# Scores of a gated linear attention: products of 64 rows, one a head, in place of pairs beside zeros

## The chip, the core and the metric

One core of a Trainium2 chip runs the whole program. The metric is the device time of one execution in microseconds. The kernel before was timed in three runs: 610.01, 610.43 and 611.85, the median being 610.43. The execution whose profile is read here took 611.44.

## What is computed

One layer of a hybrid decoder over 512 tokens of 1024 channels: a mixer (gated linear attention beside a short convolution), a mixture of 16 experts, a gate with per-layer embeddings, and a last norm, all in float32. The change lies in the attention: 4 heads, keys of 64 channels, values of 128. Cut to what matters:

```python
def step(state, inp):
    qc, kc, vc, ac = inp
    cum = jnp.cumsum(ac, axis=2)
    o_inter = jnp.einsum('bhld,bhde->bhle', qc * jnp.exp(cum), state)
    diff = cum[:, :, :, None, :] - cum[:, :, None, :, :]
    decay = jnp.exp(jnp.where(causal, diff, -jnp.inf))
    scores = jnp.einsum('bhtd,bhsd,bhtsd->bhts', qc, kc, decay)
    o_intra = jnp.einsum('bhts,bhse->bhte', scores, vc)
```

The decay differs by channel, so a score is not a plain product of q and k.

## The kernel before

Tokens stand in chunks of 128 (NT = 4). Heads are held in pairs (`pr` = 0 or 1): partitions 0 to 63 hold the one head's channels, 64 to 127 the other's, tokens along the free axis. `qT`, `kT` and `cum` are such tiles of 128x512, one a pair.

Scores are made by levels `b` = 1, 2, 4 to 64. At a level each block of 2b tokens falls into an earlier and a later half; the decay between a key of the earlier and a query of the later half goes by way of the boundary, so it is a product of a factor of the key and one of the query. `lev_sub` (POOL) takes the differences of `cum`, `lev_exp` (ScalarE) their exponentials `F`, and `lev_mul` (VectorE) multiplies the keys' halves by `kT` in place (line 537) and writes the queries' halves, times `qT`, to another tile (line 540). `scores(b, cc)` then makes the products for two of the four chunks on TensorE (line 549): the stationary operand is `F` of a chunk, 128 channels by 128 tokens, the moving one the chunk's 64 later-half queries. Since the stationary operand holds both heads of a pair, the queries are laid out as 128 columns: 64 of the one head, with zeros in the other head's partitions, and 64 of the other head, with zeros in the first one's. The tile for that, `qz`, lies in the right halves of the tiles that held x (xs in the trace), twice over for alternate levels; POOL writes its zeros once (`zero_q`, lines 495 and 496). Line 552 copies the products into the score tile `scs` under a mask (VectorE).

Two scores calls a level make 14. They don't stand alone. `merged` writes one projection step (12 products of 128x512, line 445) and then one or more of the side steps, and so sets the order by hand:

```python
merged(proj_steps([f"pC{i}" for i in range(4)], c_out), gla[:8])
merged(proj_steps([f"pu{i}" for i in range(4)], u_out), gla[8:16])
merged(proj_steps([f"pg{i}" for i in range(4)], g_out), gla[16:] + tail + [nop] * 2)
```

The first two give one side step to each projection step, the third two or three. The products of the scores, the diagonal (line 566, 2 columns) and other small ones take their PSUM banks in turn from a pool of four (`aux_ps`); a new tile waits until what read the fourth before it is done. The projections have four banks of their own.

Each projection's weights come as float32, and are split into a high and a low part by ScalarE (line 117) and VectorE (line 118): three products a weight. `Stream` holds them: a transfer starts when a slot of its ring comes free, a split when TensorE has used an earlier one (`pump`).

Three other places matter below. Line 468 (`decay1`) makes pz from an operand of 16 rows, between projections. Line 614 (`o_mm`) multiplies the state, 64 rows a head, `hf` being the half of the partitions, each half to its own bank. Line 681 (`u_out`) writes `cu` on VectorE from the projection pu; line 811 is a product of the later embedding part, where TensorE also waits for a register (line 1168). The experts (line 1111) follow the mixer.

Of the kernel before, what the change touches and what calls it, by code (L numbers as in the profile page):

```python
# [23 lines left out]
NP = 2  # L24
# [13 lines left out]
HALF = 512  # L38
# [4 lines left out]
def merged(main, side):  # L43

    done = 0
    for i, step in enumerate(main):
        step()
        while done < (i + 1) * len(side) // len(main):
            side[done]()
            done += 1  # L50
# [101 lines left out]
def hymba_layer(ctx, tc, x, p, g_mix, w_in, w_gla_gate, b_gla_gate, g_gla_out, w_conv, w_out,  # L152
# [4 lines left out]
    p, w_in, w_out = p[0, 0], w_in[0], w_out[0]  # L157
    ve, se, pe, ge, sy = nc.vector, nc.scalar, nc.tensor, nc.gpsimd, nc.sync
# [18 lines left out]
    def aux_ps(name):  # L177
        return psa.tile([P, HALF], F32, tag="aux", name=name)

    def half(i):  # L180
        return slice(i * HALF, (i + 1) * HALF)

    def tok(t):
        return slice(t * P, (t + 1) * P)
# [11 lines left out]
    def X(t):  # L196
        return xt[t // 2][:, (t % 2) * D:(t % 2 + 1) * D]
# [55 lines left out]
    def t2k(name, dt=F32):  # L253
        return t2.tile([P, HALF], dt, tag="t2", name=name)

    def txk(name, dt=F32):
        return tx.tile([P, HALF], dt, tag="tx", name=name)
# [175 lines left out]
    def proj_steps(names, done):  # L433

        ws, dst = [], []

        def step(k):
            if k == 0:
                dst.extend(mm_ps(n_) for n_ in names)
            if k % 2 == 0:  # L440
                ws.extend(W.take())
            wh, wl = ws[k]
            for c in range(4):
                for n, (a, b_) in enumerate(((wh, hTh), (wl, hTh), (wh, hTl))):
                    pe.matmul(dst[c], a[:, tok(c)], b_[:, k, :], start=(k + n == 0), stop=(k == NK - 1 and n == 2))
                if k == NK - 1:
                    done(c, dst[c])
            if k % 2:
                W.done()
                W.pump()  # L450
        return [lambda k=k: step(k) for k in range(NK)]


    qT, kT, cum = [], [], []
# [11 lines left out]
    def decay1(pr):  # L466
        pz = aux_ps(f"pz{pr}")
        pe.matmul(pz, wg[:, tok(pr)], aT, start=True, stop=True)
        ab, m = dc[pr] = txk(f"ab{pr}"), txk(f"m{pr}")
        se.activation(ab, pz, AF.Abs, bias=bgla[:, pr:pr + 1])  # L470
        ve.tensor_scalar(m, pz, bgla[:, pr:pr + 1], 0.0, op0=OP.add, op1=OP.min)

    def decay2(pr):
        ab, m = dc[pr]
        se.activation(ab, ab, AF.Exp, scale=-1.0)
        se.activation(ab, ab, AF.Ln, bias=ones[:, 0:1])
        ve.tensor_sub(m, m, ab)
        cu = t2k(f"cum{pr}")
        ve.tensor_tensor_scan(cu, cmask.rearrange("p c t -> p (c t)"), m, 0.0, op0=OP.mult, op1=OP.add)
        cum.append(cu)  # L480

    def a_all():
        pa = aux_ps("pa")
        for t in range(NT):
            a_tr(t, pa)
        ve.tensor_copy(aT, pa[:RANK, :])

    qz = [[X(2 * i + pr)[:, half(1)].rearrange("p (c h t) -> p c h t", h=2, t=64) for pr in range(NP)]
          for i in range(2)]
    two = mc.tile([P, 2], F32, name="two")  # L490

    def zero_q():
        for i in range(2):
            for pr in range(NP):
                ge.memset(qz[i][pr][0:64, :, 1, :], 0.0)
                ge.memset(qz[i][pr][64:128, :, 0, :], 0.0)
        ge.memset(two, 0.0)
        ge.memset(two[0:64, 0:1], 1.0)
        ge.memset(two[64:128, 1:2], 1.0)

    merged(proj_steps([f"qk{j}" for j in range(4)], qk_out),
           [a_all, zero_q, lambda: decay1(0), lambda: decay1(1), lambda: decay2(0), lambda: decay2(1)])

    scs = ring.tile([P, 2 * D], F32, tag="raw3", name="scs")
    sc = [scs[:, c * HALF:(c + 1) * HALF].rearrange("p (h t) -> p h t", t=P) for c in range(NT)]
    idb = ident[:, None, :].to_broadcast([P, 4, P])

    fac = {}  # L510
    lv = (1, 2, 4, 8, 16, 32, 64)

    def lview(z, b):
        return z.rearrange("p (g u b) -> p g u b", u=2, b=b)

    def later_half(z, b):
        return z.rearrange("p (c n u b) -> p c n u b", c=NT, u=2, b=b)[:, :, :, 1, :]
# [13 lines left out]
            se.activation(Fq, Fq, AF.Exp, scale=1.0 / TAU)  # L531

    def lev_mul(b):
        R = qz[lv.index(b) % 2]
        for pr in range(NP):
            fv = lview(fac[b][pr], b)
            ve.tensor_mul(fv[:, :, 0, :], fv[:, :, 0, :], lview(kT[pr], b)[:, :, 0, :])
            for hf in range(2):
                hs = slice(64 * hf, 64 * hf + 64)
                ve.tensor_mul(R[pr][hs, :, hf, :].rearrange("p c (n b) -> p c n b", b=b),  # L540
                              later_half(fac[b][pr][hs], b), later_half(qT[pr][hs], b))

    def scores(b, cc):
        R = qz[lv.index(b) % 2]
        pl = aux_ps(f"pl{b}_{cc}").rearrange("p (c h t) -> p c h t", c=2, t=64)
        for i in range(2):
            c = 2 * cc + i
            for pr in range(NP):
                pe.matmul(pl[:, i, 2 * pr:2 * pr + 2, :], fac[b][pr][:, tok(c)], R[pr][:, c], start=True, stop=True)
        for i in range(2):  # L550
            n = 64 // b
            ve.copy_predicated(sc[2 * cc + i].rearrange("p h (n u b) -> p h n u b", u=2, b=b)[:, :, :, 1, :],
                               masks[b].rearrange("p (n b) -> p n b", b=b)[:, None].to_broadcast([P, 4, n, b]),
                               pl[:, i].rearrange("p h (n b) -> p h n b", b=b))

    qk = {}

# [86 lines left out]
    def o_out(c):  # L644
        ve.scalar_tensor_tensor(to[c], to[c], ggla, osq[c], op0=OP.mult, op1=OP.mult)

    gla = [lambda: (diag_mul(0), diag_mul(1), lev_sub(1)), lambda: (lev_sub(2), lev_exp(1)),
           lambda: (diag(0), lev_sub(4), lev_exp(2), lev_mul(1)), lambda: diag(1)]
    for j, b in enumerate(lv):
        def first(j=j, b=b):  # L650
            scores(b, 0)
            if j + 2 < len(lv):
                lev_exp(lv[j + 2])
            if j + 1 < len(lv):
                lev_mul(lv[j + 1])

        def second(j=j, b=b):
            scores(b, 1)
            if j + 3 < len(lv):
                lev_sub(lv[j + 3])  # L660
        gla += [first, second]
# [364 lines left out]
    t = NT - 1  # L1026
# [451 lines left out]
    for t in range(NT):  # L1478
        n = t + 1
# [15 lines left out]
    t = NT - 1  # L1495
# [12 lines left out]
    for i, c in enumerate(cols[1:]):  # L1508
        for k in range(NK):
            (xh, xl), (wh, wl) = x2T[t][k], wq[1][k]  # L1510
            for n, (a, b_) in enumerate(((xh, wh), (xh, wl), (xl, wh))):
                pe.matmul(pgl[i][:, :256], a, b_[:, 256 * i:256 * i + 256], start=(k + n == 0),  # L1512
                          stop=(k == NK - 1 and n == 2))
# [7 lines left out]
    c = cols[2]  # L1521
# [37 lines left out]
```

## Time and profile before

| | |
|---|---|
| Median of three runs | 610.43 us (610.01 to 611.85) |
| The profiled execution's own time | 611.44 us |
| Its span, first to last instruction | 609.7 us |
| Mean granted TensorE clock | 0.992 of 2.4 GHz |
| Busy: TensorE products, its loads, VectorE, ScalarE, GpSimd | 590.3, 452.6, 480.4, 364.7, 112.6 us |
| The line of the score products | 112 records, 14.8 us, from 80.3 to 127.2 us |
| HBM read | 137.03 MB |

PE is TensorE's stream of products, PEld its loads of stationary operands, which overlap the stream; DVE is VectorE, ACT ScalarE, POOL GpSimd. The ends of products are modelled: their starts are what to read. An f32 product appears as two loads and two products, so the 56 products of line 549 appear as 112; after fp32r operands (the projections) one product is one record. A shape such as 64*128 is rows by columns of the stationary operand.

### The profile page before, as it was taken

To read this page: it belongs to the slowest core of one execution; us is meant where nothing else is said; L and a number is where in the kernel's file an instruction comes from. 1 tells how busy PE (TensorE), PEld (TensorE's weight loads), DVE (VectorE), ACT (ScalarE), POOL (GpSimd) and SP (SyncE) were. 2 spreads that over 40 slices of the span, in tenths; PEclk is the share of its full clock that TensorE was granted. 3 is DMA by queue.
4 is the path that set the end of the run, shared out by engine and by line. 5 is a ranking of instruction groups with operands and counts; after the bars stand their busy time and mean duration, and the time that the engine had idled before them with its cause. 6 is when DMAs were issued, how large, how long until landed. Compare 5 with 4: busy or idle time off the path is not lost.

```text
span 609.7 us, 8447 instructions
## 1 busy us (share of the span) xinstructions
PE 590.3 (97%) x3030; PEld 452.6 (74%) x3030; DVE 480.4 (79%) x804; ACT 364.7 (60%) x518; POOL 112.6 (18%) x147
## 2 busy tenths in 40 slices
PE   7999999999999999899999999999999999989994
PEld 6997888887687788677777777777777777666884
DVE  4742799874395476799999999999999998879763
ACT  5532537203714333678877878877787898776322
POOL 1440664100420000123210111111011100000111
PEclk9999999999999999899999999999999999999998
DMA  8632222221126958599999999999999999991001
GB/s 281 215 105 70 69 70 69 70 79 61 55 83 219 384 187 310 174 388 363 379 374 363 357 360 343 377 375 359 346 344 351 376 319 378 360 359 75 35 34 70
DMA packets 65292, 146.15 MB, mean 240 GB/s; under 512 B 5205, under 2 KB 5804, under 8 KB 65246
## 3 DMA queue, kind: packets, MB, share of 16 engines
q1 hardware_dynamic: 61342, 136.16, 61.3%
q0 software_dynamic: 3744, 9.15, 6.3%
q8 instruction: 24, 0.39, 0.2%
q10 hardware_dynamic: 160, 0.27, 0.1%
q14 instruction: 22, 0.18, 0.1%
HBM read 137.03 MB, written 12.19 MB: 245 GB/s over the span
## 4 chain that ended last, share of the span: by engine, by line
PE 53%; DVE 3%; ACT 2%; issue 1%; POOLq 0%; DVEq 0%; ACTq 0%
PE pg L1111 14%; PE pd L1111 14%; PE pu L1111 13%; PE pgate L1111 5%; PE pt_xT L1099 2%; PE pp L811 1%; PE pgate_last L1512 1%; DVE lo L113 1%; PE pt_hT L1099 1%; DVE lo L118 1%; ACT hi L112 1%; PE px L1418 1%; PE pz L1246 0%; PE pslot L926 0%; ACT L1382 0%
## 5 line engine op out<-in xcount | busy, mean ns | idle before, releaser
L113 DVE TENSOR_TENSOR lo<-raw,hi 128x1024 fp32r<-128x1024 f32 x172 | 203.3, 1218 | 14.1 <-ACT hi L112 14.0
L112 ACT CAST hi<-raw 128x1024 fp32r<-128x1024 f32 x172 | 170.5, 1053 | 0.3 <-DMA raw<-in_w_exp_up_dram 0.3
L118 DVE SCALAR_TENSOR_TENSOR lo<-raw,cst,hi 128x512 fp32r<-128x512 f32 (+1 forms) x56 | 44.8, 843 | 17.7 <-ACT hi L117 17.5
L1081 POOL DMA_INDIRECT xe<-xgd,rowi x12 | 19.4, 1613 | 165.0 <-PE pt_xT L1099 158.7
L113 DVE TENSOR_TENSOR lo<-x,hi 128x1024 fp32r<-128x1024 f32 x30 | 36.0, 1218 | 1.7 <-ACT hi L112 1.7
L117 ACT ACTIVATE hi<-raw,cst 128x512 fp32r<-128x512 f32 (+1 forms) x56 | 36.7, 717 | 0.5 <-DMA raw<-in_w_in_dram 0.5
L1132 POOL DMA_INDIRECT xd<-ye,rowi x15 | 22.5, 1501 | 49.0 <-ACT ye L1305 45.4
L112 ACT CAST hi<-x 128x1024 fp32r<-128x1024 f32 x30 | 30.8, 1052 | 0.0
L1111 PE MATMUL pg<-hi,xT_1h 128*96 128x512 f32 x60 | 24.4, 407 | 0.0
L1111 PE MATMUL pg<-hi,xT_0h 128*96 128x512 f32 x60 | 23.7, 395 | 0.0
L1111 PE MATMUL pg<-lo,xT_1h 128*96 128x512 f32 x60 | 23.6, 394 | 0.0
L1111 PE MATMUL pg<-hi,xT_1l 128*96 128x512 f32 x60 | 23.5, 392 | 0.0
L1111 PE MATMUL pg<-lo,xT_0h 128*96 128x512 f32 x60 | 23.5, 392 | 0.0
L1111 PE MATMUL pg<-hi,xT_0l 128*96 128x512 f32 x60 | 23.5, 391 | 0.0
L1111 PE MATMUL pu<-hi,xT_0h 128*96 128x512 f32 x56 | 22.9, 409 | 0.0
L1111 PE MATMUL pu<-lo,xT_0h 128*96 128x512 f32 x56 | 22.1, 395 | 0.0
L1111 PE MATMUL pu<-lo,xT_1h 128*96 128x512 f32 x56 | 22.1, 394 | 0.0
L1111 PE MATMUL pu<-hi,xT_1h 128*96 128x512 f32 x56 | 22.1, 394 | 0.0
L1111 PE MATMUL pu<-hi,xT_1l 128*96 128x512 f32 x56 | 22.0, 392 | 0.0
L1111 PE MATMUL pu<-hi,xT_0l 128*96 128x512 f32 x56 | 21.9, 392 | 0.0
L636 ACT ACTIVATE sq<-xs 128x512 f32<-128x512 f32 x4 | 2.5, 630 | 28.5 <-DVE xs L618 28.5
L728 POOL TENSOR_TENSOR xs<-xs,sg 128x128 f32<-128x128 f32 x16 | 11.3, 738 | 44.2 <-ACT sg L723 44.1
(583 smaller groups left out, 1598.0 us busy)
## 6 DMA issues: line engine op xcount, KB each, us to landing
raw<-in_w_exp_gate_dram SPq DMA_DIRECT2D x28, 1024.0 KB, 16.8
raw<-in_w_exp_down_dram SPq DMA_DIRECT2D x27, 1024.0 KB, 13.9
raw<-in_w_exp_up_dram SPq DMA_DIRECT2D x26, 1024.0 KB, 18.1
raw<-in_w_in_dram SPq DMA_DIRECT2D x10, 1024.0 KB, 5.0
x<-in_w_exp_up_dram SPq DMA_DIRECT2D x6, 1024.0 KB, 13.5
x<-in_w_exp_down_dram SPq DMA_DIRECT2D x5, 1024.0 KB, 16.0
xs<-in_x_dram SPq DMA_DIRECT2D x16, 256.0 KB, 5.6
raw<-in_w_out_dram SPq DMA_DIRECT2D x4, 1024.0 KB
```

Source lines behind the costliest of these rows:

```text
L112: self.nc.scalar.copy(hi, rw)
L113: los.append(lambda: eng.tensor_sub(lo, rw, hi.bitcast(F32)))
L117: self.nc.scalar.activation(hi[:, c_], rw[:, c_], AF.Copy, scale=g_)
L118: los.append(lambda c_=c_, g_=g_: eng.scalar_tensor_tensor(lo[:, c_], rw[:, c_], g_, hi[:, c_].bitcast(F32), op0=OP.mult, op1=OP.subtract))
L728: ge.tensor_tensor(tv, tv, sgs[i][:, tok(t)], op=OP.mult)
L811: pe.matmul(pps_[i], a[:, tok(t)], b_[:, half(ci)], start=(k + n == 0), stop=(k == 1 and n == 2))
L1081: ge.indirect_dma_start(out=x_, out_offset=None, in_=xgd, in_offset=bass.IndirectOffsetOnAxis(ap=idx, axis=0), bounds_check=S - 1, oob_is_ ...
L1099: pe.transpose(pt[:, k * n:(k + 1) * n], src[:n, tok(k)], ident[:n, :n])
L1111: pe.matmul(dst, a, b_, start=(k + n == 0), stop=(k == nk - 1 and n == 2))
L1132: ge.indirect_dma_start(out=xd, out_offset=bass.IndirectOffsetOnAxis(ap=idx, axis=0), in_=y_, in_offset=None, bounds_check=S - 1, oob_is_e ...
L1418: pe.transpose(pt[:, tok(k)], X(t)[:, ci * HALF + k * P:ci * HALF + (k + 1) * P], ident)
L1512: pe.matmul(pgl[i][:, :256], a, b_[:, 256 * i:256 * i + 256], start=(k + n == 0), stop=(k == NK - 1 and n == 2))
```

## The change

The pair's zeros go. The queries' tile becomes `qd`, 256 columns (4 chunks of 64) over all 128 partitions, written by one product a pair in place of two of 64 partitions. `scores` makes one product a head, chunk and pair of it: rows 0 to 63 of the operands into bank `pl[0]`, rows 64 to 127 into bank `pl[1]`. So a call has 8 products of 64 rows and 64 columns in place of 4 of 128 and 128, and takes two banks in place of one. The copy goes by half (all chunks and pairs of a call from one bank) in place of by chunk; there are two a call as before. `zero_q` becomes `make_two`, without the eight memsets.

```diff
-    qz = [[X(2 * i + pr)[:, half(1)].rearrange("p (c h t) -> p c h t", h=2, t=64) for pr in range(NP)]
+    qd = [[X(2 * i + pr)[:, HALF:HALF + 256].rearrange("p (c t) -> p c t", t=64) for pr in range(NP)]
           for i in range(2)]
...
-    def zero_q():
-        for i in range(2):
-            for pr in range(NP):
-                ge.memset(qz[i][pr][0:64, :, 1, :], 0.0)
-                ge.memset(qz[i][pr][64:128, :, 0, :], 0.0)
+    def make_two():
...
     def lev_mul(b):
-        R = qz[lv.index(b) % 2]
+        R = qd[lv.index(b) % 2]
...
-            for hf in range(2):
-                hs = slice(64 * hf, 64 * hf + 64)
-                ve.tensor_mul(R[pr][hs, :, hf, :].rearrange("p c (n b) -> p c n b", b=b),
-                              later_half(fac[b][pr][hs], b), later_half(qT[pr][hs], b))
+            ve.tensor_mul(R[pr].rearrange("p c (n b) -> p c n b", b=b), later_half(fac[b][pr], b),
+                          later_half(qT[pr], b))
 
     def scores(b, cc):
-        R = qz[lv.index(b) % 2]
-        pl = aux_ps(f"pl{b}_{cc}").rearrange("p (c h t) -> p c h t", c=2, t=64)
+        R = qd[lv.index(b) % 2]
+        pl = [aux_ps(f"pl{b}_{cc}_{hf}")[:, :256].rearrange("p (q t) -> p q t", t=64) for hf in range(2)]
         for i in range(2):
             c = 2 * cc + i
             for pr in range(NP):
-                pe.matmul(pl[:, i, 2 * pr:2 * pr + 2, :], fac[b][pr][:, tok(c)], R[pr][:, c], start=True, stop=True)
-        for i in range(2):
-            n = 64 // b
-            ve.copy_predicated(sc[2 * cc + i].rearrange("p h (n u b) -> p h n u b", u=2, b=b)[:, :, :, 1, :],
+                for hf in range(2):
+                    hs = slice(64 * hf, 64 * hf + 64)
+                    pe.matmul(pl[hf][:, 2 * i + pr, :], fac[b][pr][hs, tok(c)], R[pr][hs, c], start=True, stop=True)
+        n = 64 // b
+        sv = scs[:, 2 * cc * HALF:2 * (cc + 1) * HALF].rearrange("p (q h n u b) -> p q h n u b", h=2, n=n, u=2, b=b)
+        for hf in range(2):
+            ve.copy_predicated(sv[:, :, hf, :, 1, :],
                                masks[b].rearrange("p (n b) -> p n b", b=b)[:, None].to_broadcast([P, 4, n, b]),
-                               pl[:, i].rearrange("p h (n b) -> p h n b", b=b))
+                               pl[hf].rearrange("p q (n b) -> p q n b", b=b))
```

How the order moves. On TensorE, around the first level's second call, before (pl is the scores' bank, xs the tile of the queries, F the factors of one pair, pC a projection's bank):

```order
L445 MATMUL pC_772<-hTh,hi 128x512
L445 MATMUL pC_772<-hTh,lo 128x512
L445 MATMUL pC_772<-hTl,hi 128x512
L549 MATMUL pl_1_926<-xs_79,F_0_789 128x128
L549 MATMUL pl_1_926<-xs_79,F_1_792 128x128
...
L445 MATMUL pC_769<-hTh,hi 128x512
```

and with the change:

```order
L445 MATMUL pC_764<-hTh,hi 128x512
L445 MATMUL pC_764<-hTh,lo 128x512
L445 MATMUL pC_764<-hTl,hi 128x512
L545 MATMUL pl_1_0_919<-xs_79,F_0_781 128x64
L545 MATMUL pl_1_1_920<-xs_79,F_0_781 128x64
L545 MATMUL pl_1_0_919<-xs_79,F_1_784 128x64
L545 MATMUL pl_1_1_920<-xs_79,F_1_784 128x64
...
L445 MATMUL pC_761<-hTh,hi 128x512
```

Each pair's product becomes two, one to each of two banks, and the products on both sides of the call, the projections', have 128 rows where these have 64. At the marks the same rows follow once more, for the call's second chunk. Thirteen calls lie so between projections. The last level's two calls, the 13th and 14th, stand back to back, with the change as before:

```order
L445 MATMUL pg_1282<-hTl,hi 128x512
L545 MATMUL pl_0_0_1295<-xs_79,F_0_1141 128x64
...
L545 MATMUL pl_0_1_1296<-xs_79,F_1_1144 128x64
L545 MATMUL pl_1_0_1307<-xs_79,F_0_1141 128x64
...
L545 MATMUL pl_1_1_1308<-xs_79,F_1_1144 128x64
L445 MATMUL pg_1279<-hTh,hi 128x512
```

So there are thirteen stretches of score products, the last one twice as long.

On VectorE, from the first call's copies to the next ones, before:

```order
L552 COPY_PREDICATED scs<-mask_158,pl_0_893 128x256 x2
L537 TENSOR_TENSOR F_0_813<-F_0_813,qkT_746 128x128x2
L540 TENSOR_TENSOR xs_80<-F_0_813,qkT_736 64x4x64 x2
L537 TENSOR_TENSOR F_1_816<-F_1_816,qkT_751 128x128x2
L540 TENSOR_TENSOR xs_80<-F_1_816,qkT_741 64x4x64 x2
L118 SCALAR_TENSOR_TENSOR lo<-raw_672,cst,hi 128x512 x2
L552 COPY_PREDICATED scs<-mask_158,pl_1_926 128x256 x2
```

and with the change:

```order
L549 COPY_PREDICATED scs<-mask_158,pl_0_0_883 128x4x64
L549 COPY_PREDICATED scs<-mask_158,pl_0_1_884 128x4x64
L533 TENSOR_TENSOR F_0_805<-F_0_805,qkT_738 128x128x2
L534 TENSOR_TENSOR xs_80<-F_0_805,qkT_728 128x256
L533 TENSOR_TENSOR F_1_808<-F_1_808,qkT_743 128x128x2
L534 TENSOR_TENSOR xs_80<-F_1_808,qkT_733 128x256
L118 SCALAR_TENSOR_TENSOR lo<-raw_664,cst,hi 128x512 x2
L549 COPY_PREDICATED scs<-mask_158,pl_1_0_919 128x4x64
L549 COPY_PREDICATED scs<-mask_158,pl_1_1_920 128x4x64
```

Two half-height products a pair become one of full height, and nothing changes its place. ScalarE's and SyncE's rows stay in number and order; GpSimd's lose the eight memsets.

## Rows read from the trace of the kernel before

**Rows 1.** Page, part 1: busy us (share of the span) xinstructions.

```profile
PE 590.3 (97%) x3030; PEld 452.6 (74%) x3030; DVE 480.4 (79%) x804; ACT 364.7 (60%) x518; POOL 112.6 (18%) x147
```

**Rows 2.** Busy by stretches: PE, PEld, DVE, ACT, POOL (xinstructions), clock, DMA share, GB/s.

```profile
60.00:135.00 75.00, 74.53 (x387) 62.56 (x386) 65.36 (x112) 30.75 (x52) 27.36 (x36) 1.00 0.22 71
...
260.00:560.00 300.00, 296.43 (x1462) 210.59 (x1461) 278.98 (x380) 240.48 (x306) 47.84 (x30) 1.00 0.99 352
```

**Rows 3.** TensorE's waits: line, releaser, us in total, times, longest.

```profile
PE pp L811 <- DVEq L1168: 1.5, 1, 1.5
...
PE pB L445 <- ACT sg L723: 0.9, 1, 0.9
...
PE pg L445 <- DVE cu L681: 0.3, 1, 0.3
```

**Rows 4.** Timeline, PE at the second call: start us, us, engine, line, xcount.

```profile
83.75 0.39 PE L445 MATMUL pC<-hTl,hi 128*128 128x512 f32 x1
83.98 1.05 PE L549 MATMUL pl<-xs,F 128*128 128x128 f32 x8
...
84.76 0.28 PE L549 MATMUL pl<-xs,F 128*128 128x128 f32 x1
84.79 0.48 PE L445 MATMUL pC<-hTh,hi 128*128 128x512 f32 x1
85.11 0.41 PE L445 MATMUL pC<-hTh,lo 128*128 128x512 f32 x1
```

**Rows 5.** Timeline, the loads (PEld) of the same call.

```profile
83.76 1.09 PEld L549 LDWEIGHTS pl<-xs,F 128*128 128x128 f32 x8
84.76 0.19 PEld L445 LDWEIGHTS pC<-hTh,hi 128*128 128x128 f32 x1
```

**Rows 6.** Timeline, seven of the loads of the diagonal's products (2 columns).

```profile
72.92 0.86 PEld L566 LDWEIGHTS pdg<-two,qkd 128*128 128x128 f32 x7
```

**Rows 7.** Timeline, line 614: the first four and all eight; two and four loads.

```profile
141.79 0.49 PE L614 MATMUL po<-Ec,S 64*128 64x128 f32 x4
...
141.79 0.71 PE L614 MATMUL po<-Ec,S 64*128 64x128 f32 x8
...
141.78 0.19 PEld L614 LDWEIGHTS po<-Ec,S 64*128 64x128 f32 x2
...
141.78 0.30 PEld L614 LDWEIGHTS po<-Ec,S 64*128 64x128 f32 x4
```

**Rows 8.** Timeline, the entry to line 468's products of 16 rows.

```profile
50.58 0.39 PE L445 MATMUL qk<-hTl,hi 128*128 128x512 f32 x1
50.90 1.12 PE L468 MATMUL pz<-aT,wg 16*128 16x512 f32 x2
...
50.90 0.29 PEld L468 LDWEIGHTS pz<-aT,wg 16*128 16x128 f32 x2 [0.36 <-issue]
```

**Rows 9.** Timeline, the exit from line 614's last pair.

```profile
151.37 0.28 PE L614 MATMUL po<-Ec,S 64*128 64x128 f32 x2
...
151.91 0.39 PE L445 MATMUL pg<-hTh,lo 128*128 128x512 f32 x1
...
151.57 0.19 PEld L445 LDWEIGHTS pg<-hTh,hi 128*128 128x128 f32 x1
```

**Rows 10.** VectorE by line, 60 to 135 us: xcount, busy us, mean ns, idle before.

```profile
L540 DVE TENSOR_TENSOR xs<-F,qkT 64x256 f32<-64x256 f32 x28 | 16.1, 574 | 0.2
L552 DVE COPY_PREDICATED scs<-mask,pl 128x256 f32<-128x256 uint8 x28 | 12.5, 531 | 3.0 <-PE pl L549 2.9
L537 DVE TENSOR_TENSOR F<-F,qkT 128x256 f32<-128x256 f32 x14 | 7.2, 517 | 0.2
```

**Rows 11.** Line 495 on POOL: ns min/median/max, first and last start (four of eight).

```profile
L495 POOL MEMSET xs<- x4: 304/306/308, 34.4 to 36.5; 64x256 f32 x4
```

**Rows 12.** Timeline, the second and third calls' copies, and the fourth call.

```profile
89.55 2.48 DVE L552 COPY_PREDICATED scs<-mask,pl 128x256 f32<-128x256 uint8 x4
91.83 1.05 PE L549 MATMUL pl<-xs,F 128*128 128x128 f32 x8
```

**Rows 13.** Busy by stretches, columns as in rows 2: the stretch after line 811's wait.

```profile
249.00:252.50 3.50, 3.50 (x10) 2.71 (x9) 2.51 (x15) 1.69 (x5) 0.67 (x1) 0.52 0.79 214
```

More of the change, by code (lines that the diff above doesn't have):

```diff
@@ L501, in hymba_layer @@
     merged(proj_steps([f"qk{j}" for j in range(4)], qk_out),
-           [a_all, zero_q, lambda: decay1(0), lambda: decay1(1), lambda: decay2(0), lambda: decay2(1)])
+           [a_all, make_two, lambda: decay1(0), lambda: decay1(1), lambda: decay2(0), lambda: decay2(1)])
     scs = ring.tile([P, 2 * D], F32, tag="raw3", name="scs")
```

## The prediction

> **What bounds the kernel now.** I read the page's busy shares first: TensorE's products fill 97% of the span, VectorE 79% [rows 1]. Shares are averages, so next comes the view by stretches: from 60 to 135 us, where all score products lie, PE is busy for 74.53 of 75 us and VectorE for 65.36; in the experts, 260 to 560 us, PE for 296.43 of 300 [rows 2]. Then TensorE's own waits: after 60 us only a few stand there, the largest 1.5 us for a register that VectorE's chain feeds (line 1168), then 0.9 us and 0.3 us [rows 3]. So TensorE's stream sets the end, from the scores to the last expert. A microsecond added to that stream moves the end by one; a microsecond taken off VectorE moves it only where one of those waits is for VectorE. The expert weights do not soften this: their transfers start when ring slots come free, and TensorE's progress frees those.
>
> **What one call of `scores` costs TensorE today.** A 128-row call is eight records (an f32 product shows as two loads and two streams, x8 for four products). The pC product before the call starts at 83.75, the first score product at 83.98, the next pC at 84.79 and the one after it at 85.11 [rows 4]. From pC to second pC that is 1.36 us. The first of the eight starts at 83.98 and the last at 84.76, so they come every 0.11 us. The loads run ahead: the first one goes out at 83.76, while pC still streams, and the load of the next pC at 84.76, together with the last score product [rows 5]. Nothing is lost at either edge.
>
> **What paces these products.** The diagonal's products have only 2 columns, and seven loads span 0.86 us with 0.19 each, so they still come every (0.86 - 0.19) / 6 = 0.11 us [rows 6]. The load of 128 columns is the floor; a shorter stream does not lower it.
>
> **What 64-row products cost.** The kernel already has some: line 614 multiplies the state in the same order (first half, second half, first half, second half), each half to its own bank, x24 records. Four of its records end 0.49 us after the first start, eight end 0.71 us after: two pairs in 0.22, a pair every 0.11 us [rows 7]. So the two halves do run side by side. Their loads do so too: two loads take 0.19 in all, and the second pair adds 0.11 (0.30 - 0.19) [rows 7]. A load of 64 rows therefore takes as long as one of 128 rows; what is gained is that two go at once.
>
> The change's call has 16 records in 8 pairs. A pair streams 64 columns where line 614 streams 128, so its stream is half as long (0.05 us), and the load's 0.11 sets the pace. **Eight pairs at 0.11 take what eight products at 0.11 took: no gain on TensorE.** The Trainium skill, "TensorEngine Tiling (Array Packing)", section "Theoretical Speedup", would have it otherwise: up to 2 times for a dimension of 64 or less. By that rule the sum below would be 14 x 8 x 0.055 = 6.2 us lower; the loads of the diagonal and of line 614 speak against it here.
>
> **What the change of the array's shape costs.** Entry: where a pz product of 16 rows follows a stream of 128 rows, its load does not run ahead. The 128-row product starts at 50.58, pz's two loads lie from 50.90 to 51.19 with 0.19 each, so the second goes out at 51.00 as the first product begins to stream [rows 8]. That is 0.43 us after the 128-row product; in today's call it is 83.98 - 83.75 = 0.23. Entry costs 0.20 more. Exit: the last pair of line 614 starts at 151.37, the load of the next 128-row product goes out only at 151.57, and the second product after it starts at 151.91 [rows 9]: 0.54, where today it is from the last score product (84.76) to 85.11, thus 0.35. Line 614's last pair streams 128 columns; a pair of 64 saves 0.05 of that, so exit costs 0.14 more. Together 0.34 us a call. The Trainium skill, the same page, section "Key Properties", says that a change of the tiling mode, not of the tile alone, drains TensorE; it gives no price.
>
> The 14 calls form 13 islands, since the last two stand back to back and the mode doesn't change between them: 13 x 0.34 = **+4.4 us**. Bounds: if the exit saves nothing for its shorter stream, 0.39 x 13 = +5.1; if the pairs come at 0.107 rather than 0.111, the 112 pairs give back 0.4, and with an exit another 0.05 cheaper, 4.4 - 0.4 - 0.65 = +3.4 remains.
>
> **The other parts.** VectorE loses 14 instructions: 28 products of 64x256, 574 ns on average, 16.1 us, become 14 of 128x256, for which the 14 products of line 537 are the nearest row, 517 ns on average, 7.2 us [rows 10]; some 9 us less. Only the 0.3 us that TensorE waits for `cu` gains, because the last level's products stand right before the `cu` products: -0.3. The rest is cover that grows. The copies stay 28, of as many elements; now they take four 64-column pieces of one half out of one bank. If the new pattern ran at half speed, 12.5 us more [rows 10] would come to VectorE and 9 would have gone, inside the 9.6 us it has free in this stretch [rows 2]. The eight memsets on POOL (306 ns each) lie at 34 to 37 us, long before anyone reads the tiles [rows 11]: nothing.
>
> The banks: a call now holds two of four, so a call waits until the copies of the call two before are done, where four were allowed. The tightest place is the fourth call, at 91.83. The four copies from 89.55 to 92.03 belong to the second and third calls; the second's are done at about 90.8 [rows 12], 1.0 us ahead. The two removed multiplications before them add over a microsecond to that. So this wait is taken as nothing; if it bit, it would be some tenths of a call, not of all calls.
>
> **The sum.** +4.4 - 0.3 = +4.1 us. On the profiled execution, 611.44 us (span 609.7 and 1.7 around it), that is 615.5; that execution stands 1.0 above the median of the three runs, 610.43. I forecast for the median: **614.5 us**, 0.7% slower. A measurement of this kernel can tell 0.3%, 1.8 us, from no change.
>
> One piece swings by itself: after the 1.5 us wait, the granted clock is 0.52 in 249 to 252.5 us [rows 13], nearly all of it at 1.2 of 2.4 GHz, which costs about 0.48 x 3.5 = 1.7 us. The three runs, 610.01 to 611.85, spread as wide. I don't know whether a stretch that arrives 4 us later keeps it.
>
> **Rivals.**
> 1. *The edges are hidden* (no change, chance 0.07). If the drain at entry or exit ran under something that the 16-row and line-614 rows lack, only pace would count, and that is equal: 610.43 - 0.3 = 610.1. Against it: both edges show a load that waits some 0.2 us beyond the last product's start, at both kinds of place where the shape changes.
> 2. *The stream sets the pace, not the load* (faster, 0.05). If a 64-row load cost half, a pair would come every 0.056 us: 14 x 8 x 0.055 = 6.2 us less, 614.5 - 6.2 = 608.3. It decides for faster once a pair comes in under 0.058 us (4.1 + 1.8 = 5.9, over 112 pairs = 0.053 off 0.111). For it: columns are halved. Against: the diagonal's loads hold 0.11 with 2 columns. The skill's rule of 2 times is this rival.
> 3. *The halves don't run side by side here* (slower still, 0.05), so the change's pairs are none: 112 more steps of 0.11 us, +12.4, thus 627. For it: nothing but the shorter stream; line 614 has the same order and the same two banks.
>
> **How the numbers follow.** My forecast has 0.83. Its own bounds are 610.43 + 3.4 - 0.3 - 1.7 = 611.8 (cheap edges, the slow stretch gone) and 610.43 + 5.1 + 1.4 = 616.9 (dear edges, no gain at `cu`, and 1.4, as the upper of the three runs stands above their median). The three rivals with 0.17 lie outside, and some 0.03 of the forecast's tails: the range is 611.8 to 616.9. Slower by over 0.3%: 0.82 of the forecast and rival 3, 0.87. Within 0.3%: rival 1 and 0.01 of the forecast, 0.08. Faster: rival 2, 0.05.
>
> **What would show it.** In the profile after: score records 224 in place of 112, two at a time (their 16 records span about 1.0 us); the first load of a call about 0.32 us after the pC product before it, not together with it; the load of the next pC about 0.15 us after the last pair; from pC to the second pC about 1.70 us where 1.36 stood; VectorE's busy time in this stretch down by some 9 us with no gain in the span; every later stage later by about 4 us and as long as before. I would be wrong if pairs came every 0.06 us (rival 2), if the loads still ran ahead (rival 1), if the 16 records spanned 1.9 us (rival 3), or if TensorE waited for VectorE at the start of calls, the banks' doing.

## The result, and the profile after

The changed kernel takes 613.80 us in the median of six runs (613.17 to 615.83), the kernel before, in six runs beside it, 610.84 (609.66 to 611.85). The ratio is 1.0056, its 95% interval 1.0043 to 1.0069: slower by 3.4 us (2.6 to 4.2). The two medians alone stand 2.96 us apart, inside that interval. The forecast was 4.1 us.

The busy shares on the page of the changed kernel, beside [rows 1]:

```profile
PE 592.2 (97%) x3142; PEld 450.5 (74%) x3142; DVE 468.7 (77%) x790; ACT 364.9 (60%) x518; POOL 108.1 (18%) x139
```

VectorE works 11.7 us less in all, TensorE's products 1.9 more. The stretches of the changed kernel, with the columns of [rows 2]:

```profile
60.00:135.00 75.00, 75.00 (x483) 59.57 (x482) 51.72 (x94) 30.53 (x51) 25.30 (x36) 1.00 0.22 71
...
249.00:252.50 3.50, 2.01 (x15) 1.44 (x14) 1.83 (x14) 2.39 (x3) 1.88 (x2) 1.00 0.15 29
```

From 60 to 135 us TensorE now counts as never idle, and VectorE is idle for 23 of 75 us, in part because some of its work has moved past 135 us. TensorE's 75.00 hides what the change costs: the modelled end of a product reaches over the gap behind it, so what a call loses shows only in the starts. Next the timeline of TensorE's products at the second call, beside [rows 4]:

```profile
83.64 0.40 PE L445 MATMUL pC<-hTl,hi 128*128 128x512 f32 x1
83.97 1.11 PE L545 MATMUL pl<-xs,F 64*128 64x64 f32 x16
85.01 0.50 PE L445 MATMUL pC<-hTh,hi 128*128 128x512 f32 x1
85.35 0.40 PE L445 MATMUL pC<-hTh,lo 128*128 128x512 f32 x1
```

and of its loads, beside [rows 5]:

```profile
83.97 0.97 PEld L545 LDWEIGHTS pl<-xs,F 64*128 64x128 f32 x16 [0.37 <-issue]
85.00 0.19 PEld L445 LDWEIGHTS pC<-hTh,hi 128*128 128x128 f32 x1
```

From pC to second pC it is 85.35 - 83.64 = 1.71 us, where 1.36 stood. The sixteen loads go out two at a time, (0.97 - 0.19) / 7 = 0.11 us a pair. The first load no longer runs ahead: it comes 0.33 us after pC. At the other edge pC's load goes out at 85.00, 0.19 after the last pair (83.97 + 1.11 - 0.27 = 84.81).

TensorE's waits of the changed kernel, beside [rows 3]:

```profile
PE pp L808 <- DVEq L1165: 1.5, 1, 1.5
...
PE pB L445 <- ACT sg L720: 0.9, 1, 0.9
...
PE pg L1108 <- DVE xT0al L1088: 0.3, 1, 0.3
```

The wait for `cu` is gone; one of 0.3 us at the first expert has come.

Where the time went is best read between two marks on TensorE: the first pC product, with which the stage of the scores begins, and the first pB product, which follows its tail. In the kernel before:

```profile
64.51 0.40 PE L445 MATMUL pC<-hTh,hi 128*128 128x512 f32 x1
...
160.09 0.49 PE L445 MATMUL pB<-hTh,hi 128*128 128x512 f32 x1 [0.93 <-ACT sg L723]
```

and in the changed one:

```profile
64.05 0.40 PE L445 MATMUL pC<-hTh,hi 128*128 128x512 f32 x1
...
163.16 0.49 PE L445 MATMUL pB<-hTh,hi 128*128 128x512 f32 x1 [0.93 <-ACT sg L720]
```

95.58 us have become 99.11: **+3.53 us in this stage**, which accounts for the difference of the runs (2.6 to 4.2). The two profiled spans alone, 609.7 and 611.3, would mislead. The changed kernel's execution was 0.46 us earlier before the stage began, and after it the granted clock stays at 1.00 in 249 to 252.5 us, where the one before fell to 0.52 [rows 13]: from the first pp product to the first expert's transpositions it takes 241.89 to 257.24, 15.35 us, where 238.82 to 255.71, 16.89, stood. Of thirteen kernels profiled in this study two show some 16.9 there and eleven 15.3, with and without the change.

### The profile page after: what moved, and what is told of

Its sections match the earlier page's. It is cut to its first block, busy times and chain, and to the rows that moved or that the text cites. A ratio compares the mean times of both kernels' runs of the same rounds, so it can differ in the third digit from the quotient of the medians.

```text
span 611.3 us, 8659 instructions
## 1 busy us (share of the span) xinstructions
PE 592.2 (97%) x3142; PEld 450.5 (74%) x3142; DVE 468.7 (77%) x790; ACT 364.9 (60%) x518; POOL 108.1 (18%) x139
## 4 chain that ended last, share of the span: by engine, by line
PE 52%; DVE 4%; ACT 1%; issue 1%; POOLq 0%; DVEq 0%; ACTq 0%
PE pg L1108 14%; PE pd L1108 14%; PE pu L1108 13%; PE pgate L1108 5%; PE pt_xT L1096 2%; DVE lo L113 1%; PE pgate_last L1509 1%; PE pt_hT L1096 1%; DVE lo L118 1%; ACT hi L112 1%; PE px L1415 1%; PE pz L1243 0%; PE pslot L923 0%; ACT L1379 0%; ACT ye L1302 0%
## 5 line engine op out<-in xcount | busy, mean ns | idle before, releaser
L118 DVE SCALAR_TENSOR_TENSOR lo<-raw,cst,hi 128x512 fp32r<-128x512 f32 (+1 forms) x56 | 43.3, 817 | 18.6 <-ACT hi L117 18.6
L549 DVE COPY_PREDICATED scs<-mask,pl 128x256 f32<-128x256 uint8 x28 | 13.0, 531 | 16.8 <-PE pl L545 16.6
```

The lines of the kernel that those rows point to most:

```text
L118: los.append(lambda c_=c_, g_=g_: eng.scalar_tensor_tensor(lo[:, c_], rw[:, c_], g_, hi[:, c_].bitcast(F32), op0=OP.mult, op1=OP.subtract))
L549: ve.copy_predicated(sv[:, :, hf, :, 1, :], masks[b].rearrange("p (n b) -> p n b", b=b)[:, None].to_broadcast([P, 4, n, b]), pl[hf].rearra ...
```

## The experiments

Every run has a kernel before beside it on its chip. The stage is the time from the first pC to the first pB product in that run's trace; where two kernels do the same in this stage it agrees to some 0.02 us (95.58 in the kernel before and in b_pad, 94.67 and 94.66 in b_early and b_both), which is much finer than the runs' medians. It comes from one trace a kernel. For b_vector it is the only ground, since its ratio's interval reaches 1.0.

| run | median us | ratio to before, 95% interval | stage us, against before |
|---|---|---|---|
| changed kernel | 613.80 | 1.0056 (1.0043 to 1.0069) | 99.11, +3.53 |
| a_seven | 612.25 | 1.0027 (1.0017 to 1.0037) | 97.57, +1.99 |
| a_amid | 620.22 | 1.0158 (1.014 to 1.0177) | 105.55, +9.97 |
| b_amid | 613.07 | 1.0039 (1.0025 to 1.0054) | 98.02, +2.44 |
| a_wide | 614.64 | 1.007 (1.005 to 1.009) | 99.81, +4.23 |
| b_rows64 | 614.08 | 1.0056 (1.0038 to 1.0074) | 99.09, +3.51 |
| b_vector | 609.97 | 0.999 (0.9981 to 1.0) | 94.66, -0.92 |
| a_apart | 620.98 | 1.0171 (1.0154 to 1.0189) | 105.66, +10.07 |
| a_twos | 614.43 | 1.0069 (1.0045 to 1.0093) | 99.74, +4.16 |
| b_pad | 609.71 | 0.9984 (0.9974 to 0.9994) | 95.58, 0.00 |
| b_early | 609.60 | 0.9984 (0.9974 to 0.9994) | 94.67, -0.91 |
| b_both | 608.83 | 0.9968 (0.9957 to 0.998) | 94.66, -0.92 |

**Fewer edges (a_seven).** Both calls of a level in one side step:

```diff
             scores(b, 0)
+            scores(b, 1)
...
-            scores(b, 1)
```

> The changed kernel with both calls of a level back to back: 7 stretches of score products in place of 13. Edge theory (each stretch costs TensorE 0.34 us for entry and exit): 6 x 0.34 = 2.0 us less than the changed kernel, 613.8 - 2.0 = 611.8, unless TensorE then waits for the copies, since a level holds all four banks. Rival, the cost lies in the pairs themselves (3.5 us over 112 pairs): no change, 613.8.

The stage fell by 1.54 us of the 2.0 expected: the cost follows the number of stretches, so the pairs are not its cause. Most of the rest shows at the first level, and its times point to the banks, which one call does not feel and two in a row do. The first level's TensorE rows of a_seven:

```profile
79.94 0.39 PE L445 MATMUL pC<-hTl,hi 128*128 128x512 f32 x1
80.25 2.41 PE L545 MATMUL pl<-xs,F 64*128 64x64 f32 x32
82.59 0.50 PE L445 MATMUL pC<-hTh,hi 128*128 128x512 f32 x1
82.93 0.40 PE L445 MATMUL pC<-hTh,lo 128*128 128x512 f32 x1
```

and VectorE's there:

```profile
80.17 1.27 DVE L565 TENSOR_TENSOR scs<-ident,pdg 128x512 f32<-128x512 f32 x2
```

The other levels' 32 records take 2.59 us from projection to second projection, these 2.99. The second call needs the two banks of the diagonal's products, and VectorE reads those until 81.44, in the middle of the stretch. No run took this wait away, so the banks are argued here and not shown. That 0.40 leaves 0.1 of the 6 x 0.34 = 2.04 without a name.

**More edges (a_amid, b_amid).** One product of 128 rows and 2 columns after a call's first chunk, in the changed kernel and in the one before. This is a_amid's, in part; b_amid puts the two columns where the second chunk's product is then written:

```diff
+            if i == 0:
+                pe.matmul(bank[0][:, 256:258], fac[b][0][:, tok(c)], two, start=True, stop=True)
```

> The changed kernel with one product of 128 rows and 2 columns amid each call, whose result nobody reads: 14 more exits and entries. The product itself is two records at 0.11, 0.22 us a call, 3.1 us in all. Edge theory: exit (0.20 from the last pair to the next load, and 0.11 for that load, less 0.11) and entry after a short stream (0.09 drain) add about 0.28 a call, thus 14 x (0.22 + 0.28) = 7.0 us over the changed kernel, 620.8. Rival (no cost at the edges): 3.1 us, 616.9.

> The kernel before with the same product of 128 rows and 2 columns amid each call, whose result nobody reads: the price of the product without a change of rows. All theories: 14 x 0.22 = 3.1 us over the kernel before, 613.9.

a_amid's stage is 6.44 us over the changed kernel's, where 7.0 were forecast and 3.1 by the rival. Its timeline at the second call:

```profile
84.73 0.40 PE L445 MATMUL pC<-hTl,hi 128*128 128x512 f32 x1
85.06 0.66 PE L546 MATMUL pl<-xs,F 64*128 64x64 f32 x8
85.65 0.38 PE L548 MATMUL pl<-two,F 128*128 128x2 f32 x2
85.97 0.66 PE L546 MATMUL pl<-xs,F 64*128 64x64 f32 x8
86.56 0.50 PE L445 MATMUL pC<-hTh,hi 128*128 128x512 f32 x1
86.90 0.40 PE L445 MATMUL pC<-hTh,lo 128*128 128x512 f32 x1
```

From pC to second pC it is 2.17 us, 0.46 more than the changed kernel's 1.71. The two records cost 0.22 of that (in b_amid, where the rows don't change, a call takes 1.58 us in place of 1.36), the new exit and entry 0.24 where 0.28 was estimated. b_amid's stage became 2.44 us longer, less than the 3.1 forecast, because its later TensorE also lost most of the two waits of the kernel before, of which more below: the third call takes 1.59 us there, the twelfth 1.86.

**Is the stream or the load the pace (a_wide).** Streams of 128 columns in the changed kernel (in part: the banks' shape and the copies' operand change with it):

```diff
-                    pe.matmul(pl[hf][:, 2 * i + pr, :], fac[b][pr][hs, tok(c)], R[pr][hs, c], start=True, stop=True)
+                    pe.matmul(pl[hf][:, 2 * i + pr], fac[b][pr][hs, tok(c)], R[pr][hs, 2 * cc:2 * cc + 2],
+                              start=True, stop=True)
```

> The changed kernel with streams of 128 columns in place of 64 (both chunks' queries each time); the scores of every second chunk are then those of the other chunk's queries. Load theory (the load of 128 columns paces the pairs at 0.11 us): pairs as before, the last pair of a stretch ends 0.05 later, 13 x 0.05 = 0.7 us over the changed kernel, 614.5. Rival (the stream paces): pairs every 0.22, 112 x 0.11 = 12 us more, 626.

Twice the columns cost 0.70 us in the stage, 0.05 a stretch, as expected. Its timeline:

```profile
84.44 0.40 PE L445 MATMUL pC<-hTl,hi 128*128 128x512 f32 x1
84.77 1.16 PE L545 MATMUL pl<-xs,F 64*128 64x128 f32 x16
85.86 0.50 PE L445 MATMUL pC<-hTh,hi 128*128 128x512 f32 x1
86.20 0.40 PE L445 MATMUL pC<-hTh,lo 128*128 128x512 f32 x1
```

1.76 us from pC to second pC, where streams of 64 take 1.71. So 64 columns hide behind the loads, and what the change halves was not the bound. Rival 2 falls.

The 0.05 lies at the entry. The products up to the second one or pair, in the kernel before, the changed one and a_wide:

```profile
83.98 0.38 PE L549 MATMUL pl<-xs,F 128*128 128x128 f32 x2
...
83.97 0.44 PE L545 MATMUL pl<-xs,F 64*128 64x64 f32 x4
...
84.77 0.49 PE L545 MATMUL pl<-xs,F 64*128 64x128 f32 x4
```

With 0.27 us for the last record, the second one starts 0.34, 0.50 and 0.55 us after its pC product (83.75, 83.64, 84.44). From the last pair to the second pC it is 0.54 us in the changed kernel and in a_wide alike.

That the 0.11 is the load's, and not a fixed price of a product, is borne out by line 624 of the kernel before, whose stationary operand has 64 columns. All its loads and those of line 549 (ns, shortest/median/longest, first and last start):

```profile
L624 PEld LDWEIGHTS pd<-v,kdT x24: 132/137/137, 137.1 to 148.7; 128*64 128x64 f32 x24
...
L549 PEld LDWEIGHTS pl<-xs,F x112: 186/192/192, 80.1 to 127.1; 128*128 128x128 f32 x112
```

Half the stationary columns take 55 ns less, half of 0.11 us. No run made score products with fewer stationary columns.

**One part of the change at a time (b_rows64, b_vector).** TensorE's part with the old tile (b_rows64, here beside the changed kernel's product):

```diff
-                    pe.matmul(pl[hf][:, 2 * i + pr, :], fac[b][pr][hs, tok(c)], R[pr][hs, c], start=True, stop=True)
+                    pe.matmul(pl[hf][:, 2 * i + pr, :], fac[b][pr][hs, tok(c)], R[pr][hs, c, hf], start=True, stop=True)
```

and VectorE's part with 128-row products (b_vector, beside the product of the kernel before):

```diff
-                pe.matmul(pl[:, i, 2 * pr:2 * pr + 2, :], fac[b][pr][:, tok(c)], R[pr][:, c], start=True, stop=True)
+                pe.matmul(pl[:, i, 2 * pr:2 * pr + 2, :], fac[b][pr][:, tok(c)], R[pr][:, 2 * cc:2 * cc + 2], start=True, stop=True)
```

> TensorE's part alone: products of 64 rows in two banks and copies by half, but the queries in the old tile, with the zeros' memsets and 28 half-height products on VectorE as before. Theory A (two waits of TensorE for VectorE, 0.45 us at the third call and 0.5 us after the twelfth, vanish because VectorE has less to do): they stay here, 13 x 0.34 = 4.4 us over the kernel before, 615.2. Theory B (they vanish because TensorE itself comes later to each call): as the changed kernel, 3.5 us over the kernel before, 614.3.

> VectorE's part alone: one product a pair and no zeros, as in the change, while TensorE makes the 128-row products of 128 columns of before, on the queries of both chunks; the scores are then sums over two heads. Theory A (VectorE's lighter load ends the two waits): 0.95 us under the kernel before, 609.9. Theory B (only a later TensorE ends them): as the kernel before, 610.8.

In the stage b_rows64 gave +3.51, as theory B has it, and b_vector -0.92, as theory A has it. Both theories hold, each for its part. VectorE's lighter load ends the two waits when it comes alone; in the change it adds nothing, since TensorE, 0.34 us later with every stretch, would have lost them anyhow. The parts don't add: 3.51 - 0.92 is not 3.53.

The two waits, in the kernel before. TensorE at the third call:

```profile
87.46 0.39 PE L445 MATMUL pC<-hTl,hi 128*128 128x512 f32 x1
87.69 0.38 PE L549 MATMUL pl<-xs,F 128*128 128x128 f32 x2
88.29 0.91 PE L549 MATMUL pl<-xs,F 128*128 128x128 f32 x6 [0.21 <-issue]
...
89.27 0.39 PE L445 MATMUL pC<-hTh,lo 128*128 128x512 f32 x1
...
121.14 0.40 PE L445 MATMUL pu<-hTl,hi 128*128 128x512 f32 x1
...
122.69 0.47 PE L445 MATMUL pg<-hTh,hi 128*128 128x512 f32 x1 [0.26 <-DVE cu L681]
123.00 0.39 PE L445 MATMUL pg<-hTh,lo 128*128 128x512 f32 x1
```

and VectorE there:

```profile
86.56 1.62 DVE L540 TENSOR_TENSOR xs<-F,qkT 64x256 f32<-64x256 f32 x2
```

The third call stops after its first pair's product until VectorE has written the second pair's queries, at 86.56 + 1.62 = 88.18. From projection to second projection it takes 1.81 us and the twelfth call's 1.86, where the others take 1.36: 0.45 and 0.50 us. The view of waits shows 0.2 and 0.3 of them, because the modelled end of a product covers the first part of the idle time behind it: at the third call the first two records count as busy until 87.69 + 0.38 = 88.07.

**What running side by side is worth (a_apart, a_twos).** The order of a call's products:

```diff
-        for i in range(2):
-            c = 2 * cc + i
-            for pr in range(NP):
-                for hf in range(2):
-                    hs = slice(64 * hf, 64 * hf + 64)
+        for hf in range(2):
+            hs = slice(64 * hf, 64 * hf + 64)
+            for i in range(2):
+                c = 2 * cc + i
+                for pr in range(NP):
```

a_twos moves `hf` by one loop only, between `i` and `pr`.

> The changed kernel with a call's eight products in another order: the four of the first half, then the four of the second. If two halves run side by side only where they follow each other in the program, 15 steps of 0.11 in place of 8, 14 x 7 x 0.11 = 11 us over the changed kernel, 624.6; this is the price of rival 3. If TensorE finds the pairs by itself: 613.8.

> The changed kernel with the products of a chunk in the order first half, first half, second half, second half. If TensorE runs a later product of the other half ahead of up to some four records that wait (as the run with the halves one after the other suggests: 12 steps a call, not 15), at most one step a call is lost: 14 x 0.11 = 1.6 us over the changed kernel or less, 613.8 to 615.4. Rival (only neighbours pair): 13 steps a call in place of 8, 7.8 us, 621.6.

a_apart met neither: 6.54 us over the changed kernel, where 11 and 0 were expected. Its loads at the first call, by their count up to three points in time:

```profile
80.23 0.52 PEld L545 LDWEIGHTS pl<-xs,F 64*128 64x128 f32 x4 [0.36 <-ACT hi L117]
...
80.23 1.02 PEld L545 LDWEIGHTS pl<-xs,F 64*128 64x128 f32 x12 [0.36 <-ACT hi L117]
...
80.23 1.47 PEld L545 LDWEIGHTS pl<-xs,F 64*128 64x128 f32 x16 [0.36 <-ACT hi L117]
```

Four go alone, (0.52 - 0.19) / 3 = 0.11 us each; then eight within 0.50, two at a time; then four alone in 0.45. Loads of one half alone come every 0.11 us, so the eight must be of both halves. That is 12 steps, 4 more than in pairs, or 0.44 us; a call alone between projections takes 0.49 us more (2.20 for 1.70), and 0.05 of that has no name. The last level's two calls together lose only 0.61, since there the first call's second half also meets the first half of the next call: 12 x 0.49 + 0.61 = 6.5 us. So TensorE takes up a waiting product of the other half past several of its own, but not past all eight records. a_twos was formed on that: 0.63 us over the changed kernel, under the 1.6 allowed and far from 7.8.

**Fewer edges elsewhere (b_pad).** pz over 128 rows, the rest zero, in the kernel before:

```diff
-    wg = mc.tile([RANK, 256], F32, name="wg")
+    wg = mc.tile([P, 256], F32, name="wg")
+    ve.memset(wg, 0.0)
...
-    aT = txk("aT")[:RANK, :]
+    aT = txk("aT")
+    ge.memset(aT, 0.0)
```

> The kernel before with pz's two products (line 468) over 128 rows, those beyond 16 being zero on both sides: two entries and exits fewer elsewhere in the program. Edge theory: entry 0.20 and exit about 0.19 each time, 2 x 0.39 = 0.8 us under the kernel before, 610.0. Rival (the edge's cost there belongs to the long f32 stream, not to the change of rows): 610.8.

TensorE there:

```profile
50.66 0.39 PE L447 MATMUL qk<-hTl,hi 128*128 128x512 f32 x1
50.89 1.02 PE L470 MATMUL pz<-aT,wg 128*128 128x512 f32 x2
...
51.98 0.39 PE L447 MATMUL qk<-hTh,lo 128*128 128x512 f32 x1
```

1.32 us from qk to second qk. The kernel before takes 1.71, from 50.58 [rows 8] to its second qk:

```profile
52.29 0.40 PE L445 MATMUL qk<-hTh,lo 128*128 128x512 f32 x1
```

The qk stage, from its first product to the first pC, takes 24.55 us in place of 25.33: 0.78 less, as expected. So the price belongs to the change of rows, not to the score products.

**A version that beats both (b_early, b_both).** In the kernel before, the next level's products ahead of the first call's copies on VectorE; b_both adds b_pad's edit. In part (`scores` makes no copies any more, `score_copies` does, and the second call's copies stay right behind it):

```diff
             if j + 1 < len(lv):
                 lev_mul(lv[j + 1])
+            score_copies(b, 0)
```

> The kernel before with the next level's products on VectorE put ahead of the copies of a level's first call, so that they fill the time in which VectorE waits for that call. If the two waits (0.45 us at the third call, 0.5 us after the twelfth) come from these products being late on VectorE, both go, and TensorE's stage from the first pC to the first pB is 0.95 us shorter: 610.5 - 0.95 = 609.5. Rival (the waits belong to VectorE's total load in that stage): no change, 610.5.

> The kernel before with that order and with pz's products over 128 rows: two measured gains in different stages, 0.95 and 0.78 us of TensorE's stream. If they add, 610.5 - 1.7 = 608.8, a ratio of 0.997 to the kernel before. Rival (the earlier qk stage only moves VectorE's lateness along): 0.8 less, 609.7.

Both waits go (-0.91 in the stage), and the two gains add: b_both takes 608.83 us, where 608.8 were forecast, a ratio of 0.9968 (0.9957 to 0.998) to the kernel before. Its computation is the kernel's own, in another order and with zero rows.

## Why the prediction was right, and where not

The time, 613.80 us, lies in the range of 611.8 to 616.9, and the direction and the mechanism stood. One term of the sum was too small.

*The pace.* "Eight pairs at 0.11 take what eight products at 0.11 took": the trace after has pairs every 0.11, and a_wide shows that the stream is not what sets it.

*The edges.* 0.34 us a call were forecast, 1.70 from pC to second pC; 1.71 came. Its split was different. I took 0.05 off the exit for the shorter stream; in the trace the exit takes as long as line 614's (84.81 to 85.35, 0.54), 0.19 more than before, and it is the entry that costs less, 0.50 - 0.34 = 0.16 in place of 0.20. So the 0.05 for the shorter stream was right in size and stood at the wrong edge, which the sum doesn't show. Thirteen stretches, not fourteen calls, was right: twelve calls lie alone between projections, and the last two together cost one entry and exit.

*The step that was mis-sized* is the gain set against it, "Only the 0.3 us that TensorE waits for `cu` gains". It was 0.95: 0.45 at the third call, which the list of TensorE's waits showed as no more than 0.2 and which I left out, and 0.50 after the twelfth, shown as 0.3. With 13 x 0.34 = 4.4 less 0.95 the sum is +3.5, and 3.53 were measured. The reason that I gave, VectorE's lighter load, would do it alone (b_vector) but wasn't needed (b_rows64): a TensorE that comes later to each call loses the waits too.

*The cover.* VectorE's products fell from 16.1 us [rows 10] to 6.7, and the copies by half cost the same as by chunk, 531 ns each, as the changed kernel's rows by line show (60 to 140 us):

```profile
L549 DVE COPY_PREDICATED scs<-mask,pl 128x256 f32<-128x256 uint8 x28 | 13.0, 531 | 16.8 <-PE pl L545 16.6
L534 DVE TENSOR_TENSOR xs<-F,qkT 128x256 f32<-128x256 f32 x14 | 6.7, 475 | 0.0
```

It became idle time: before the copies VectorE now waits 16.6 us for TensorE, where it waited 2.9. In all VectorE works 11.7 us less and not the 9 forecast, since records that the change leaves alone became shorter too (the 22 splits of line 118 in that time take 887 ns on average, where 953 stood); why, no run here shows. The banks made no wait in the change: the calls alone between projections all take 1.69 to 1.71 us. With two calls in a row at the first level they probably would, as a_seven's times say.

*The rivals.* Rival 1 fell with the trace after and the four runs that add or remove edges; rival 2 with a_wide. Rival 3 did not occur; its 12.4 us are more than even a_apart's order costs, 6.54, since TensorE finds pairs by itself over some distance.

## What to carry to other kernels

Splitting a product into two of half the rows wins nothing while the load of the stationary operand is the pace: two half loads side by side take as long as one whole (shown here for moving operands of 64 and of 128 columns). What it adds is an entry and an exit, 0.34 us here, each time the rows of the products change in TensorE's stream, so put such products in few long stretches, or fill up the rows of small ones with zeros (b_pad won 0.39 us a product at pz). Work taken off an engine beside the bound is worth only the waits that it ends, and a slower bound ends the same waits; read such a wait from start to start of the products, not from the list of waits.

## What was not expected of the hardware

Two halves of the array pair even when the program does not put them next to each other: with four products (eight records) of the one half ahead of the other's, the second half's first load went out once five of the first's eight had gone, at the start of each of a_apart's thirteen stretches. And the granted clock's short fall to half (1.2 GHz), 3.4 us long near 250 us and worth 1.5 us there, came in the profiles of two kernels out of thirteen, the kernel before and b_early. All thirteen have the wait of 1.5 us ahead of it, so why these two fell no run here shows.
